# Turning a head's second negated maxima behind the next head's first scores, and rounding sample queries in fewer operations

## The chip, the cores and the metric

The kernel runs on one core of a Trainium2 chip. A core has TensorE (matmuls; its weight loads are listed apart as PEld), VectorE (DVE), ScalarE (ACT), GpSimd (POOL) and SyncE (SP), which here only issues DMAs. Each engine works through its own instructions in order; engines wait for each other by semaphores. Matmul results land in PSUM, everything else lies in SBUF or in DRAM. The metric is the device time of one execution in microseconds (us); the time before is the median of three runs.

## What is computed

One inference step of a trunk of two layers, for a prompt of 1024 positions and for 8 samples of 8 new positions each: a Mamba-2 layer, then a layer of multi-head latent attention (MLA), with the same weights for both groups. The change lies in the attention layer. For the prompt, with 16 heads, a latent of 256 and a rotary part of 32:

```python
def latent_partial(q_lat, q_pe, ckv, kpe, mask):
    s = (jnp.einsum('bqhc,bkc->bhqk', q_lat, ckv.astype(F32))
         + jnp.einsum('bqhr,bkr->bhqk', q_pe.astype(F32), kpe.astype(F32))) * MLA_SCALE
    if mask is not None:
        s = jnp.where(mask, s, NEG_INF)
    m = jnp.max(s, axis=-1)
    p = jnp.exp(s - m[..., None])
    return m, jnp.sum(p, axis=-1), jnp.einsum('bhqk,bkc->bhqc', p, ckv.astype(F32))
```

The samples use the same function over 16 pages of an old cache and their own new positions. Their queries in latent form are `absorb(q_nope, w_uk)`, a product with a head's 64 x 256 weights, beside the rotary part `q_pe`.

## The kernel before

**Number format.** Most operands of matmuls are written as a sum of two parts in a rounded 32-bit format (fp32r): `split` (L129, L130) has ScalarE round a source into the high part, and VectorE subtract it from the source into the low part. A product then takes three matmuls: high by high, low by high, high by low.

**Prompt heads.** `mla_heads` loops over 16 heads h. For each head there are 12 steps t; step t scores one block of 128 keys against a half qc of the queries (512): four steps for the first half, eight for the second. `qk` (L1246 to L1253) computes the transposed scores in PSUM (tile st, two buffers), and ScalarE takes the exponential twice, once rounded (th) and once in full (P); VectorE or GpSimd writes their difference tl (L1260). `pv` (L1277 to L1279) multiplies by the values two steps later.

The exponential needs the maximum of each query subtracted. This is done inside the score matmul: rows 96 and 97 of the transposed queries (qTh) hold the negated maxima as two parts, and the keys have ones there. So, one head ahead, `maxpass(h + 1, qc)` computes coarse scores (tile sc, L1214), and VectorE reduces them (L1217, L1219), negates the maxima (L1225, L1226, tile nm), TensorE turns them (L1229, tile nmp), VectorE copies the result to SBUF (L1231, nr), and two DMAs on SP's queue carry it through DRAM (L1233, nd) into rows 96 and 97 of qTh (L1234). `qk` of step t = 0 needs the rows of the first half, that of t = 4 those of the second.

**Units between the steps.** Beside `qk` and `pv`, each step takes some units of other work from a list: 6 units of `maxpass(h + 1, 0)` (a), 10 of `maxpass(h + 1, 1)` (b), and 4 to 16 of `prep(h + 2)` merged evenly into it: for every fourth head the values of four heads (vp), for every second the keys (kp), and for each head the query transposes (qT), the sample queries' transposes (qs) and the sample product (ql). The list is spread over the 12 steps: `while done < total * (t + 1) // 12`. The last two units of b are the negation and the turn. Within a step the order is `qk`, then units, then `pv` of two steps before.

**Sample queries.** In `prep_q` (L1176 to L1200) TensorE transposes a head's 64 sample queries (96 rows: 64 plain, 32 rotary) and the head's weights into one PSUM tile (qs). VectorE copies the queries (qsn, L1182), ScalarE the weights (wt, L1184). One unit later TensorE multiplies both (L1188, tile ql) and the two halves of the latent are split one after the other into qlh and qll. The rotary part goes from qsn into qpr in three copies: high, high again, low (L1197 to L1199).

**What sets the order.** In this stage the instructions of TensorE and GpSimd run in the order in which the program writes them. The order on VectorE, ScalarE and SP's queue is laid out ahead of time by a planner with a cost model. Tiles with several buffers are reused as soon as their readers are done; readers of one PSUM tile on different engines take turns. The PSUM tiles of the units share four buffers (tag sc). The gate of a head (gt, L1271) and the results (og_d, L1292) use SP's queue too.

Of the kernel before, what the change touches and what calls it, by code (L numbers as in the profile page):

```python
# [8 lines left out]
F32 = mybir.dt.float32  # L9
F32R = mybir.dt.float32r  # L10
AF = mybir.ActivationFunctionType
ALU = mybir.AluOpType
# [7 lines left out]
NT = 8  # L20
# [106 lines left out]
def split(k, hi, lo, src, eng=None):  # L127
    nc = k.nc
    nc.scalar.copy(hi, src)  # L129
    (eng or nc.vector).tensor_tensor(lo, src, hi.bitcast(F32), op=ALU.subtract)  # L130
# [895 lines left out]
class Heads:  # L1026
# [136 lines left out]
    def prep_q(self, h):  # L1163
        k, nc, sp = self.k, self.k.nc, self.sp
        hg, pr, j = h // 4, h // 2, h % 2
        if j == 0:
            self.load_q(pr)
        qh, ql = self.q_of(h)
        for c in range(2):
            p = self.wt(f"qT{h}{c}")  # L1170
            for i in range(4):
                nc.tensor.transpose(p[:96, i * 128 : i * 128 + 128], self.qt[:, 4 * c + i, 96 * j : 96 * j + 96], k.ident)
            cs = slice(512 * c, 512 * c + 512)
            split(k, qh[:96, cs], ql[:96, cs], p[:96])
            yield
        p = self.wt(f"qs{h}")  # L1176
        nc.tensor.transpose(p[:96, :64], self.qt[:64, 8, 96 * j : 96 * j + 96], k.ident[:64, :64])
        for c in range(2):
            nc.tensor.transpose(p[:64, 128 + c * 128 : 256 + c * 128],
                                self.wkr[:, c, 64 * (h % 4) : 64 * (h % 4) + 64], k.ident)  # L1180
        qsn = sp.tile([96, 64], F32, tag="qsn", name=f"qsn{h}", bufs=2)
        nc.vector.tensor_copy(qsn, p[:96, :64])  # L1182
        wt = sp.tile([64, 256], F32, tag="wt", name=f"wt{h}", bufs=2)
        nc.scalar.copy(wt, p[:64, 128:384])  # L1184
        yield
        pl = self.wt(f"ql{h}p")
        for c in range(2):
            nc.tensor.matmul(pl[:, c * 64 : c * 64 + 64], wt[:, c * 128 : c * 128 + 128], qsn[0:64],  # L1188
                             start=True, stop=True)
        for c in range(2):  # L1190
            src = pl[:, c * 64 : c * 64 + 64].rearrange("p (b t) -> p b t", t=NT)
            dh = k.qlh[:, c].rearrange("p b (h t) -> p b h t", t=NT)[:, :, h]
            dl = k.qll[:, c].rearrange("p b (h t) -> p b h t", t=NT)[:, :, h]
            split(k, dh, dl, src)
        src = qsn[64:96].rearrange("p (b t) -> p b t", t=NT)
        qv = k.qpr.rearrange("p b (h t) -> p b h t", t=NT)[:, :, h]
        nc.vector.tensor_copy(qv[0:32], src)  # L1197
        nc.vector.tensor_copy(qv[32:64], src)
        nc.vector.tensor_tensor(qv[64:96], src, qv[0:32].bitcast(F32), op=ALU.subtract)  # L1199
        yield  # L1200

    def maxpass(self, h, qc):
        k, nc, sp = self.k, self.k.nc, self.sp
# [96 lines left out]
def merge(*lists):  # L1300
    z = [((i + 0.5) / len(x), n, u) for n, x in enumerate(lists) for i, u in enumerate(x)]
    return [u for _, _, u in sorted(z, key=lambda e: e[:2])]


def mla_heads(k, hd, sm, early, st):
    k.tc.keep_in_program_order(k.nc.scalar.preload_act_table_set("natural_log_exp_and_others"))
    held, late = [], []

    def step(g):
        try:  # L1310
            next(g)
        except StopIteration:
            pass

    for h in range(MH):
        units = []
        if h == MH - 2:
            early.close()
            sm.begin(st, hd.psum)
        if h + 1 < MH:  # L1320
            a, b = hd.maxpass(h + 1, 0), hd.maxpass(h + 1, 1)
            units += [a] * 4 + [b, a, b, b, b, a] + [b] * 6
        if h + 2 < MH:
            g = hd.prep(h + 2)
            units = merge(units, [g] * hd.units(h + 2))
        if h + 2 == MH:
            g = sm.prefetch()
            units[PF:PF] = [g] * 2
            units += [g] * 2
        if h + 1 == MH:  # L1330
            sm.preload()
            flow = sm.flow()
            units = [flow] * FLOW
        total, done = len(units), 0
        for t in range(12):
            qc, jb = (0, t) if t < 4 else (1, t - 4)
            held.append((h, qc, jb, *hd.qk(h, qc, jb)))
            while done < total * (t + 1) // 12:
                step(units[done])
                done += 1  # L1340
            if len(held) > LEAD:
                hd.pv(*held.pop(0))
    for x in held:
        hd.pv(*x)
    return flow
# [447 lines left out]
def layer_mla(k):  # L1793
# [3 lines left out]
    with ExitStack() as st:  # L1797
# [29 lines left out]
        with tc.manual_schedule(engines={nc.tensor.engine, nc.gpsimd.engine}):  # L1827
            flow = mla_heads(k, hd, sm, early, st)
# [64 lines left out]
```

## Time and profile before

| | |
|---|---|
| time before, median of 3 runs | 2104.4 us (2102.95 to 2106.95) |
| span of the profiled execution, first to last instruction | 2095.4 us |
| mean granted TensorE clock over the span | 0.969 |
| instructions | 33766 |
| busy in the span: TensorE, weight loads, VectorE, ScalarE, GpSimd | 1948.3, 1763.6, 1340.1, 1043.3, 851.9 us |
| prompt heads, from the first head's first scores to the last head's steps | 1433 to 1815 us |

The profiled execution's own total time isn't listed beside its span; its span is 9.0 us shorter than the median of the runs.

A row of the profile in order of time reads: start, duration, engine, line, operation, tile written <- tiles read, shapes, count, and in brackets how long the engine was idle before it and what ended that. A row of a group reads: line, engine, operation, tiles, shapes, count, then busy time and mean duration in ns, then the engine's idle time before these instructions and what ended most of it. In a view of one tile, the last lines say for whom the engine sat idle before the tile's instructions (us, times). A row of a stretch gives its length, the busy time and count of each engine, the granted clock (1.00 is full speed) and what the DMAs did.

### The profile page before, as it was taken

Reading aid. Unit: us, or ns where it says so; the run is one execution under the profiler, and the core shown is the slowest. Engines: PE = TensorE matmul, PEld = TensorE weight load, DVE = VectorE, ACT = ScalarE, POOL = GpSimd, SP = SyncE. Lnnn points to the kernel's source line nnn. Section 1 sums busy time; section 2 is a strip of 40 time slices with the busy share of each in tenths; the row PEclk is TensorE's granted clock in tenths of the full one; section 3 lists DMA queues with packets and bytes.
Section 4 is the critical chain, followed back from the end, with each engine's and each line's share of the span. In section 5 each row is a group of like instructions: output and inputs, shape, how many; then the busy total and the mean of one; then the engine's idle time right before and its main releaser. Section 6 shows DMA issues by size and latency. Waiting matters only on the chain.

```text
span 2095.4 us, 33766 instructions
## 1 busy us (share of the span) xinstructions
PE 1948.3 (93%) x12001; PEld 1763.6 (84%) x12001; DVE 1340.1 (64%) x2838; ACT 1043.3 (50%) x2287; POOL 851.9 (41%) x1059
## 2 busy tenths in 40 slices
PE   6999999999999999789998999699999999889998
PEld 5898999899999998677787998698888888778887
DVE  4558676767676767865334314366787778776665
ACT  5455565556565656522114323234676667755552
POOL 0337564646664646744000001102343334765541
PEclk9999999999999999889999999899999989999999
DMA  4222324231324241635534342132111112464451
GB/s 144 56 59 64 111 66 115 56 114 57 105 66 115 56 115 46 208 122 192 183 124 133 124 152 63 52 108 68 48 55 52 43 37 61 133 197 131 142 152 40
DMA packets 187631, 207.61 MB, mean 99 GB/s; under 512 B 23260, under 2 KB 153064, under 8 KB 187080
## 3 DMA queue, kind: packets, MB, share of 16 engines
q1 hardware_dynamic: 182408, 185.67, 29.2%
q0 software_dynamic: 4976, 19.66, 3.0%
q8 instruction: 95, 1.56, 0.3%
q14 instruction: 72, 0.59, 0.1%
q10 hardware_dynamic: 80, 0.13, 0.0%
HBM read 152.10 MB, written 53.28 MB: 98 GB/s over the span
## 4 chain that ended last, share of the span: by engine, by line
PE 33%; DVE 9%; issue 4%; POOL 4%; DMA 3%; ACT 2%; SPq 0%; POOLq 0%; DVEq 0%; ACTq 0%
PE pq L100 5%; PE pob L100 5%; PE pj L88 4%; PE poa L100 2%; POOL kvl L1541 2%; PE pk L100 1%; PE p L100 1%; PE vp L88 1%; PE st L1246 1%; DVE tl L1260 1%; PE st L1248 1%; PE st L1247 1%; PE o L1277 1%; PE sc L1214 1%; PE kp L88 1%
## 5 line engine op out<-in xcount | busy, mean ns | idle before, releaser
L88 PE MATMUL pj<-xh,wih 128*128 128x384 f32 (+1 forms) x768 | 254.9, 336 | 10.9 <-ACT xh L235 6.6
L88 PE MATMUL pj<-xl,wih 128*128 128x384 f32 (+1 forms) x768 | 255.9, 333 | 0.0
L88 PE MATMUL pj<-xh,wil 128*128 128x384 f32 (+1 forms) x768 | 255.1, 332 | 0.0
L1260 POOL TENSOR_TENSOR tl<-P,th 128x384 fp32r<-128x384 f32 (+1 forms) x96 | 90.7, 945 | 181.0 <-ACT P L1258 138.5
L88 PEld LDWEIGHTS pj<-xh,wih 128*128 128x128 f32 x768 | 145.8, 191 | 12.5 <-ACT xh L235 7.5
L468 DVE SCALAR_TENSOR_TENSOR acc<-raw,vec,acc 128x1112 f32<-128x1112 f32 x96 | 147.0, 1535 | 11.9 <-ACT acc L465 11.1
L88 PEld LDWEIGHTS pj<-xh,wil 128*128 128x128 f32 x768 | 146.3, 190 | 0.6
L88 PEld LDWEIGHTS pj<-xl,wih 128*128 128x128 f32 x768 | 146.1, 190 | 0.5
L575 DVE TENSOR_SCALAR M<-M,tok 128x128 f32<-128x128 f32 (+1 forms) x288 | 116.6, 462 | 43.0 <-DMA M<-acs_d 35.7
L100 PE MATMUL pz<-wih,xh 128*128 128x256 f32 x504 | 143.0, 287 | 0.0
L100 PE MATMUL pz<-wil,xh 128*128 128x256 f32 (+1 forms) x504 | 142.8, 287 | 0.0
L1257 ACT ACTIVATE th<-st 128x512 fp32r<-128x512 f32 x192 | 94.1, 490 | 73.6 <-PE st L1253 54.7
L100 PE MATMUL pz<-wih,xl 128*128 128x256 f32 x448 | 128.1, 286 | 0.0
L130 DVE TENSOR_TENSOR wil<-wraw,wih 128x512 fp32r<-128x512 f32 x88 | 70.4, 802 | 65.7 <-ACT wih L129 63.1
L1541 POOL TENSOR_TENSOR kvl<-pgr,kvh 128x1024 fp32r<-128x1024 f32 x32 | 78.2, 2445 | 67.8 <-ACT kvh L1540 67.8
L100 PEld LDWEIGHTS pz<-wih,xh 128*128 128x128 f32 x504 | 96.0, 190 | 1.1
L577 ACT ACTIVATE M<-M 128x512 f32<-128x512 f32 (+1 forms) x72 | 43.8, 608 | 102.0 <-DVE M L575 101.7
L1258 ACT ACTIVATE P<-st 128x512 f32<-128x512 f32 x192 | 93.2, 486 | 0.0
L100 PEld LDWEIGHTS pz<-wil,xh 128*128 128x128 f32 (+1 forms) x504 | 92.9, 184 | 0.3
L663 POOL TENSOR_TENSOR y<-y,nw 128x256 f32<-128x256 f32 (+1 forms) x72 | 64.5, 896 | 70.2 <-ACT xD L662 69.7
L582 PEld LDWEIGHTS py<-xdt,M 128*128 128x128 f32 (+1 forms) x576 | 70.4, 192 | 19.8 <-DVE xdt L555 6.5
L100 PEld LDWEIGHTS pz<-wih,xl 128*128 128x128 f32 x448 | 85.4, 191 | 0.4
(819 smaller groups left out, 6461.6 us busy)
## 6 DMA issues: line engine op xcount, KB each, us to landing
wraw<-in_ssd_w_in SPq DMA_DIRECT2D x92, 256.0 KB
M<-acs_d SPq DMA_DIRECT2D x64, 256.0 KB
s<-in_state_ssm SPq DMA_DIRECT2D x32, 256.0 KB
y_d<-y SPq DMA_DIRECT2D x64, 128.0 KB
out_s_ssm<-s SPq DMA_DIRECT2D x32, 256.0 KB
wraw<-in_ssd_w_out SPq DMA_DIRECT2D x16, 512.0 KB
q_d<-qt SPq DMA_DIRECT2D x32, 192.0 KB
qp<-q_d SPq DMA_DIRECT2D x8, 768.0 KB
```

The lines of the kernel that those rows point to most:

```text
L88: nc.tensor.matmul(out, a, b, start=(i == 0), stop=(i == n - 1))
L100: nc.tensor.matmul(o, a, b, start=(j == 0), stop=(j == len(ops) - 1))
L130: (eng or nc.vector).tensor_tensor(lo, src, hi.bitcast(F32), op=ALU.subtract)
L468: nc.vector.scalar_tensor_tensor(acc, raw[:, j : j + n], k.convw[j][:, blk : blk + 1], acc, op0=ALU.mult, op1=ALU.add)
L575: nc.vector.tensor_scalar(M[:m, h, :m], M[:m, h, :m], tk[:, 0, 4 * g + h : 4 * g + h + 1], 0.0, op0=ALU.subtract, op1=ALU.min)
L577: nc.scalar.activation(M[:m, :, :m], M[:m, :, :m], AF.Exp)
L582: nc.tensor.matmul(py[:m, h * 64 : h * 64 + 64], M[:m, h, :m], xdt[:m, h * 64 : h * 64 + 64], start=True, stop=True)
L663: nc.gpsimd.tensor_tensor(y[:m], y[:m], nw[:m], op=ALU.mult)
L1257: nc.scalar.activation(th[:, :n], ps[:, :n], AF.Exp, scale=SCALE)
L1258: nc.scalar.activation(P[:, :n], ps[:, :n], AF.Exp, scale=SCALE)
L1260: eng.tensor_tensor(tl[:, :n], P[:, :n], th[:, :n].bitcast(F32), op=ALU.subtract)
L1541: nc.gpsimd.tensor_tensor(rl, raw, rh.bitcast(F32), op=ALU.subtract)
```

## The change

Two edits. The last unit of `maxpass(h + 1, 1)`, which turns the second half's negated maxima and sends them on, leaves the list of units: the list is one unit shorter, and the generator is kept (`turn`) and taken one step further in the next head, just after that head's first `qk`. And `prep_q` takes the rotary part straight from PSUM with one `split`, splits both halves of the latent in one operation each, and leaves the second copy of the rotary high part to one copy for all heads, issued at the start of head 14 (`rope_queries`).

```diff
-        qsn = sp.tile([96, 64], F32, tag="qsn", name=f"qsn{h}", bufs=2)
-        nc.vector.tensor_copy(qsn, p[:96, :64])
+        qsn = sp.tile([64, 64], F32, tag="qsn", name=f"qsn{h}", bufs=2)
+        nc.vector.tensor_copy(qsn, p[:64, :64])
+        qv = k.qpr[:, :, NT * h : NT * h + NT]
+        split(k, qv[0:32], qv[64:96], p[64:96, :64].rearrange("p (b t) -> p b t", t=NT))
         wt = sp.tile([64, 256], F32, tag="wt", name=f"wt{h}", bufs=2)
         nc.scalar.copy(wt, p[:64, 128:384])
         yield
...
-            nc.tensor.matmul(pl[:, c * 64 : c * 64 + 64], wt[:, c * 128 : c * 128 + 128], qsn[0:64],
+            nc.tensor.matmul(pl[:, c * 64 : c * 64 + 64], wt[:, c * 128 : c * 128 + 128], qsn,
                              start=True, stop=True)
-        for c in range(2):
-            src = pl[:, c * 64 : c * 64 + 64].rearrange("p (b t) -> p b t", t=NT)
-            dh = k.qlh[:, c].rearrange("p b (h t) -> p b h t", t=NT)[:, :, h]
-            dl = k.qll[:, c].rearrange("p b (h t) -> p b h t", t=NT)[:, :, h]
-            split(k, dh, dl, src)
-        src = qsn[64:96].rearrange("p (b t) -> p b t", t=NT)
-        qv = k.qpr.rearrange("p b (h t) -> p b h t", t=NT)[:, :, h]
-        nc.vector.tensor_copy(qv[0:32], src)
-        nc.vector.tensor_copy(qv[32:64], src)
-        nc.vector.tensor_tensor(qv[64:96], src, qv[0:32].bitcast(F32), op=ALU.subtract)
+        src = pl[:, :128].rearrange("p (c b t) -> p c b t", c=2, t=NT)
+        split(k, *(x[:, :, :, NT * h : NT * h + NT] for x in (k.qlh, k.qll)), src)
         yield
+
+    def rope_queries(self):
+        k, nc = self.k, self.k.nc
+        nc.scalar.copy(k.qpr[32:64], k.qpr[0:32].bitcast(F32))
...
-    held, late = [], []
+    held, turn = [], iter(())
...
-        units = []
+        units, b = [], iter(())
         if h == MH - 2:
             early.close()
+            hd.rope_queries()
             sm.begin(st, hd.psum)
         if h + 1 < MH:
             a, b = hd.maxpass(h + 1, 0), hd.maxpass(h + 1, 1)
-            units += [a] * 4 + [b, a, b, b, b, a] + [b] * 6
+            units += [a] * 4 + [b, a, b, b, b, a] + [b] * 5
...
             held.append((h, qc, jb, *hd.qk(h, qc, jb)))
+            if t == 0:
+                step(turn)
+                turn = b
```

## The prediction

> **What bounds the kernel now.** I read the page's first lines, then the stretch from 1433 to 1790 us, in which the heads run, by engine, then TensorE's idle time there, then single boundaries between heads in order of time. Page and busy time by stretch (columns: length, then PE, PEld, DVE, ACT, POOL busy, granted clock, DMA share, GB/s):
>
> ```profile
> PE 1948.3 (93%) x12001; PEld 1763.6 (84%) x12001; DVE 1340.1 (64%) x2838; ACT 1043.3 (50%) x2287; POOL 851.9 (41%) x1059
> ...
> 1433.00:1790.00 357.00, 334.22 (x1845) 289.36 (x1844) 280.44 (x696) 241.34 (x547) 129.85 (x126) 0.95 0.18 51
> ```
>
> TensorE is busy 334 of 357 us, VectorE 280, ScalarE 241: TensorE's program order is the clock of this stage, and its 23 idle us are what an edit can win. The view of the tile nmp (the turned maxima) on TensorE says where they are:
>
> ```profile
> L1229 PE MATMUL nmp<-ident,nm x29: 269/273/377, 1459.9 to 1788.7; 128*8 128x128 f32 x29
> its engine sat idle before it (us, times) until:
>   DVE nm L1226: 14.2, 11
>   DVE qll L130: 3.2, 4
> ```
>
> So 17.4 of the 23 us stand in front of one 0.27 us transpose, once at each of the 15 head boundaries (11 + 4). One boundary, TensorE then VectorE:
>
> ```profile
> 1476.43 0.44 PE L1214 MATMUL sc<-kTh,qTh 96*128 96x512 f32 x1
> ...
> 1478.47 0.28 PE L1253 MATMUL st<-mr 128*128 128x128 f32 x1
> 1480.78 0.27 PE L1229 MATMUL nmp<-ident,nm 128*8 128x128 f32 x1 [2.04 <-DVE nm L1226]
> 1480.81 0.42 PE L1277 MATMUL o<-th,Vh 128*128 128x384 f32 x1
> ...
> 1481.41 0.40 PE L1246 MATMUL st<-qTh,kTh 98*128 98x512 f32 x1
> 1481.65 0.40 PE L1247 MATMUL st<-qTl,kTh 98*128 98x512 f32 x1
> ...
> 1482.23 0.42 PE L1214 MATMUL sc<-kTh,qTh 96*128 96x128 f32 x1
> ```
> ```profile
> 1479.22 0.76 DVE L1219 CUSTOM_DVE_ANT_0 sc<-sc,mk,mx 128x512 f32<-128x512 f32 x1
> ...
> 1480.56 0.16 DVE L1226 SCALAR_TENSOR_TENSOR nm<-mx,nm 128x4 fp32r<-128x4 f32 x1
> ```
>
> The last score of the pass is ready at 1476.87, but VectorE, behind, takes it at 1479.22, and the transpose waits. What follows it, a value product (1480.81 to 1481.41) and the next head's first scores (to 1482.23), needs nothing of it.
>
> Idle time here costs twice. Stretches at half clock:
>
> ```profile
> 1482.10:1488.90 6.80, 6.80 (x30) 6.68 (x29) 3.74 (x10) 4.20 (x9) 1.93 (x2) 0.50 0.07 20
> 1512.80:1516.20 3.40, 3.40 (x14) 3.11 (x13) 1.26 (x4) 1.27 (x3) 0.00 (x0) 0.50 0.01 2
> 1577.70:1581.10 3.40, 3.40 (x13) 3.11 (x12) 0.92 (x4) 1.08 (x2) 0.00 (x0) 0.50 0.01 2
> 1669.80:1680.10 10.30, 9.79 (x39) 9.40 (x40) 5.14 (x18) 4.42 (x10) 2.28 (x2) 0.50 0.05 16
> 1704.00:1707.40 3.40, 3.40 (x15) 3.19 (x14) 1.22 (x5) 1.51 (x4) 0.00 (x0) 0.50 0.00 1
> 1724.40:1731.30 6.90, 6.59 (x21) 5.91 (x22) 1.77 (x7) 2.52 (x7) 1.31 (x2) 0.51 0.02 4
> ```
>
> Between 1455 and 1790 these six, 34.2 us, are all there is below full clock, and each begins within 2 us of such a wait (1480.78, 1511.35 and 1702.17 are quoted). The price:
>
> ```profile
> 1513.20 0.63 PE L1247 MATMUL st<-qTl,kTh 98*128 98x512 f32 x1
> 1513.63 0.63 PE L1248 MATMUL st<-qTh,kTl 98*128 98x512 f32 x1
> ```
>
> Start to start 0.43 us where 1481.41 to 1481.65 took 0.24: about 0.45 of such a stretch is lost, 15.4 us in all.
>
> **The change, part by part.**
>
> *The transpose behind the next head's first scores.* Same instructions, later place. It now comes after the value product (0.60) and the scores (0.82), 1.42 us of cover. The list of units is also one shorter and is spread again over the 12 steps. Three kinds of boundary follow.
>
> - h = 0, 4, 8, 12 (the four that wait for qll): the last score stays in step 10, the cover exceeds the wait of 0.8 (3.2 in four). Gone: −3.2.
> - h odd, seven: the last score moves from step 10 to step 11, just before the value product, so the cover counts from its end. From the rows: reading it 0.76, two negations of 0.16, some 0.2 between them, 1.3 us against 1.4. Nothing remains if VectorE is free; if it is still 2.35 us behind (1476.87 to 1479.22), some 2.3 remain, as now. What held it up there goes in part with the second edit; I take a remainder of 0.5 at h = 1, 5, 9, where VectorE also splits weights, and 0.2 at the other four, 2.3 in all (bounds 0 and 16). h = 14 likewise loses its small wait. These eight have 17.4 − 3.2 − 3 × 0.85 = 11.65 now, so −11.65 + 2.3 = −9.4.
> - h = 2, 6, 10: here the query transposes, the maxima's transpose and the sample product stand in a row:
>
> ```profile
> 1510.09 0.41 PE L1179 MATMUL qs<-ident,w 128*64 128x128 f32 x2
> 1511.35 0.27 PE L1229 MATMUL nmp<-ident,nm 128*8 128x128 f32 x1 [0.85 <-DVE nm L1226]
> 1511.58 0.66 PE L1188 MATMUL ql4p<-qsn,wt 64*128 64x64 f32 x4
> ...
> 1606.20 0.27 PE L1229 MATMUL nmp<-ident,nm 128*8 128x128 f32 x1 [0.85 <-DVE nm L1226]
> ...
> 1702.17 0.27 PE L1229 MATMUL nmp<-ident,nm 128*8 128x128 f32 x1 [0.85 <-DVE nm L1226]
> ```
> ```profile
> 1510.92 0.21 DVE L1182 COPY qsn<-qs 96x64 f32<-96x64 f32 x1
> 1511.16 0.36 ACT L1184 COPY wt<-qs 64x256 f32<-64x256 f32 x1 [0.71 <-DVE qsn L1182]
> 1441.53 0.58 ACT L129 CAST kTh<-kp 64x512 fp32r<-64x512 f32 x1 [3.23 <-DVE kTl L130]
> ```
>
> Take the transpose away and the sample product still waits for wt, which ends at 1511.52. Idle is not 0.85 but 1.08, before the second edit.
>
> *Its DMAs.* The store and the load of the row (SP's queue) move back by the same 1.4 us:
>
> ```profile
> 1556.08 0.27 PE L1229 MATMUL nmp<-ident,nm 128*8 128x128 f32 x1 [0.80 <-DVE qll L130]
> ...
> 1556.69 0.27 SPq L1233 DMA_DIRECT2D nd<-nr  x1
> 1557.90 0.22 SPq L1234 DMA_DIRECT2D qTh<-nd  x1
> 1562.59 0.45 SPq L1271 DMA_DIRECT2D gt<-g_d  x1
> ...
> 1556.71 0.40 PE L1246 MATMUL st<-qTh,kTh 98*128 98x512 f32 x1
> ...
> 1562.30 0.40 PE L1246 MATMUL st<-qTh,kTh 98*128 98x512 f32 x1
> ```
>
> The store lands 1.2 us after its issue (the load waits for it); give the load the same. From a transpose 0.8 behind the head's start at 1556.71: 0.6 to the store's issue (1556.08 to 1556.69 now), 1.2, 1.2, so 3.8 us; the rows are first used at 1562.30, 5.6 us behind the start. Slack 1.8: priced 0. The scores of the first half, which read the same tile meanwhile, did so before as well.
>
> *Sample queries.* For each head VectorE loses the two casts of the rotary part and one of two latent differences; the rotary difference reads PSUM now. ScalarE trades two latent casts for one of double width and a rotary one. From the groups (busy us, mean ns), one of the casts and the difference:
>
> ```profile
> L1199 DVE TENSOR_TENSOR qpr<-qsn,qpr 32x64 fp32r<-32x64 f32 x14 | 10.0, 712 | 0.4
> ...
> L1197 DVE CAST qpr<-qsn 32x64 fp32r<-32x64 f32 x14 | 7.6, 542 | 0.5
> ```
>
> With the difference cut to qsn's 0.21, 14 x (0.71 − 0.21 + 0.54), 14.6 us or about one per head leaves VectorE, and more with the rest. It had 77 idle us anyway, so it counts only in the backlog above. But ScalarE's wt now stands behind a copy and a difference on the same PSUM tile. Such readers take turns here: the cast at 1441.53 reads other partitions than the difference it waits for. So qsn, copy, difference, wt run in a chain. The two new links cost some 0.2 each by qsn's 0.21, with handovers 0.5 to 0.6. At h = 2, 6, 10 this is on TensorE's path: idle 1.6 instead of 0.85, 3 × 0.75 = +2.3. Elsewhere value products and scores stand between.
>
> [...]
>
> *The one copy for all heads at h = 14,* 32 x 1024 on ScalarE: at most the 1.05 us of
>
> ```profile
> L1540 ACT CAST kvh<-pgr x1: 1051/1051/1051, 1785.6 to 1785.6; 128x1024 fp32r<-128x1024 f32 x1
> ```
>
> ScalarE idles longer than that around a head's start; if not, +1. Taken: 0.
>
> *The clock.* Four stretches follow boundaries that lose their wait: 6.8 + 3.4 + 10.3 + 6.9 = 27.4 us, × 0.45 = −12.3. The two of 3.4 at h = 2 and 10 stay, and with 1.6 us idle I take three of 5.1: (15.3 − 6.8) × 0.45 = +3.8.
>
> **Sum:** −3.2 − 9.4 + 2.3 − 12.3 + 3.8 = −18.8. The span is 2095.4, 9.0 below the median of 2104.4; the profiled execution's own total isn't shown, and I carry the 9.0 over: 2085.6.
>
> **Rivals.**
>
> 1. *The waits go, the clock doesn't follow* (0.18). Speaks for it: several waits of 0.8 to 1.3 us have no half clock behind them. Against: none of the six stretches stands without one. Then −18.8 + 8.5 = −10.3: 2094. [...]
> 2. *The wait moves along* (0.13). VectorE stays behind, the later last score eats the cover, and the seven odd heads keep their wait behind the first scores. Then only −3.2 + 2.3 remains, and the clock as before or +3.8: 2103 to 2107.
> 3. *The rows come late* (0.12), the slower side. SP's queue is in order; if the load is put behind the gate's load, which waited until 1562.59, it is issued at 1563.04 and lands at 1564.25, 1.95 us after the scores want it. The odd heads and h = 14, 15 have no projection before that point: 9 × 1.95 = 17.6, and half clock after such waits by up to 3.1 each (6.8 × 0.45), say 14. That turns −18.8 into +13: 2117. It decides as soon as the path of 3.8 us grows by more than 1.8. Against: the gate's load becomes possible over 4 us after the row's load in the rows above.
> 4. *Nothing remains, and the clock stays full* (0.05): −17.4 − 15.4 gives 2072.
>
> **How the numbers follow.** My forecast has 0.52, own range 2078 to 2093. The range 2071 to 2106 takes in rivals 1, 4 and most of 2 and leaves out 3. About 0.2% (4.2 us) can be told from no change: faster 0.52 + 0.18 + 0.05; of rival 2 most is no change, with 0.02 on either side: faster 0.77, same 0.09, slower 0.14.
>
> **What would show it.** In the new profile the tile nmp has almost no idle time before it; ql waits for wt at three boundaries by 1.6 us; half clock is left only behind those; the first scores of each second half wait for no DMA; the rotary rows are gone from VectorE. I am wrong if TensorE idles before nmp behind the first scores, or before the scores of step 4, or if half clock appears without idle time ahead of it.

## The result, and the profile after

The changed kernel takes 2081.15 us (median of four runs, 2076.63 to 2084.15), the kernel before 2103.68 beside it (2101.3 to 2106.95): a ratio of 0.9898, 95% interval 0.9877 to 0.9919. The prediction was 2085.6. A second set of runs gave 2080.1 against 2097.64, 0.9924 (0.9901 to 0.9947). The time came out as forecast; the experiments show that most of the gain has another source than the prediction said.

The page of the kernel after, and the stretch from its first head's first scores to its last head's (columns as before: length, busy time of PE, PEld, DVE, ACT, POOL, granted clock, DMA):

```profile
PE 1939.1 (93%) x12001; PEld 1750.3 (84%) x12001; DVE 1325.8 (64%) x2790; ACT 1043.0 (50%) x2288; POOL 852.6 (41%) x1059
...
1428.87:1771.47 342.60, 327.83 (x1843) 281.31 (x1843) 264.76 (x651) 242.30 (x550) 130.38 (x126) 0.97 0.20 53
```

The same stretch of the kernel before:

```profile
1433.42:1790.45 357.03, 334.25 (x1845) 289.42 (x1845) 280.05 (x694) 241.72 (x549) 129.85 (x126) 0.95 0.18 51
```

The stage is 14.4 us shorter: TensorE's idle time falls from 22.8 to 14.8 (−8.0), its busy time, for the same matmuls, by 6.4: less half clock. The span (2077.3) is 18.1 shorter; 4.6 of it lie ahead of the first head, where of all that changed only the sample queries of the first two heads are prepared. In the second profile of the same kernel the heads begin at 1432.28 and take 340.2, so at least 3.4 of those 4.6 belong to the execution, not to the change.

Behind what TensorE waits now, from the waits of the kernel after in that stretch (us in total, times, longest), and the tile nmp:

```profile
PE sc L1212 <- DVE mx L1217: 3.5, 1, 3.5
PE st L1244 <- ACT P L1256: 2.0, 2, 1.7
PE st L1244 <- DMA qTh<-nd: 1.9, 3, 0.7
PE ql8p L1190 <- ACT wt L1186: 1.8, 1, 1.8
PE ql12p L1190 <- ACT wt L1186: 1.8, 1, 1.8
PE ql4p L1190 <- ACT wt L1186: 1.8, 1, 1.8
PE nkp L1408 <- DVE nk L1405: 0.7, 1, 0.7
PE o L1277 <- POOL tl L1258: 0.7, 1, 0.7
...
PE nmp L1227 <- DVE nm L1224: 0.2, 1, 0.2
```

The longest wait, 3.5 us in the first head, is the same in the kernel before (3.5 there, too). Of 17.4 us in front of the maxima's transpose, 0.2 are left. In their place stand 5.5 before three sample products, 1.9 behind DMAs at three first scores of a head, and near the end some 0.7 to 2 each behind ScalarE, VectorE and GpSimd. One of the three sample products, and the chain ahead of it, in order of time on TensorE, VectorE and ScalarE:

```profile
1500.78 0.41 PE L1179 MATMUL qs<-ident,w 128*64 128x128 f32 x2
1503.02 0.65 PE L1190 MATMUL ql4p<-qsn,wt 64*128 64x64 f32 x4 [1.84 <-ACT wt L1186]
```
```profile
1501.77 0.21 DVE L1182 COPY qsn<-qs 64x64 f32<-64x64 f32 x1
1502.35 0.22 DVE L130 TENSOR_TENSOR qpr<-qs,qpr 32x64 fp32r<-32x64 f32 x1
```
```profile
1502.02 0.20 ACT L129 CAST qpr<-qs 32x64 fp32r<-32x64 f32 x1 [0.88 <-DVE qsn L1182]
1502.60 0.36 ACT L1186 COPY wt<-qs 64x256 f32<-64x256 f32 x1 [0.38 <-DVE qpr L130]
```

The four readers of the tile stand in a row, as the prediction had it, and the weights are last. The stretches at half clock in the kernel after:

```profile
1437.00:1440.40 3.40, 3.40 (x11) 2.85 (x11) 1.87 (x7) 1.01 (x3) 3.34 (x5) 0.50 0.46 98
1505.30:1508.70 3.40, 3.40 (x17) 3.37 (x17) 1.73 (x6) 2.27 (x5) 0.64 (x1) 0.50 0.04 7
1594.00:1600.80 6.80, 6.80 (x27) 6.36 (x27) 2.02 (x7) 2.22 (x5) 0.13 (x1) 0.50 0.01 4
1686.20:1693.00 6.80, 6.58 (x24) 6.15 (x25) 1.86 (x6) 2.17 (x6) 0.00 (x0) 0.50 0.01 1
```

The first has its like in the kernel before (at 1441). The other three, 17.0 us instead of 34.2, begin within 2.3 us of the end of one of the three waits of 1.84. In the second profile of this kernel (the run c1 below) two of the three have half clock behind them, 13.7 us in all, and the third, just as long, has none. Last, a wait that was not foreseen, TensorE and then SP's queue:

```profile
1558.98 0.27 PE L1227 MATMUL nmp<-ident,nm 128*8 128x128 f32 x1
1565.81 0.47 PE L1244 MATMUL st<-qTh,kTh 98*128 98x512 f32 x1 [0.65 <-DMA qTh<-nd]
```
```profile
1557.36 0.39 SPq L1159 DMA_DIRECT2D qp<-q_d  x1
...
1560.30 0.43 SPq L1231 DMA_DIRECT2D nd<-nr  x1
1564.18 0.25 SPq L1232 DMA_DIRECT2D qTh<-nd  x1
```

Those are the rows of the first half. Their store stands behind the load of new queries (qp, 768 KB in the list of DMA issues) and takes 3.9 us to the next issue, where the rows of the second half took 1.2. In the kernel before the same two issues were 4.9 us apart, at the boundary that the prediction shows (its first scores start at 1481.41):

```profile
1473.04 0.42 SPq L1233 DMA_DIRECT2D nd<-nr  x1
...
1477.94 0.25 SPq L1234 DMA_DIRECT2D qTh<-nd  x1
```

There the scores came 3.5 us behind the load's issue; without the 2.04 us before the transpose it would have been 1.4, less than the 1.6 (1564.18 to 1565.81) that the load takes here.

### The profile page after: what moved, and what is told of

Same layout as the page of the kernel before. It is cut to its first block, busy times and chain, and to the rows that moved or that the text cites. A ratio compares the mean times of both kernels' runs of the same rounds, so it can differ in the third digit from the quotient of the medians.

```text
span 2077.3 us, 33714 instructions
## 1 busy us (share of the span) xinstructions
PE 1939.1 (93%) x12001; PEld 1750.3 (84%) x12001; DVE 1325.8 (64%) x2790; ACT 1043.0 (50%) x2288; POOL 852.6 (41%) x1059
## 4 chain that ended last, share of the span: by engine, by line
PE 58%; DVE 15%; DMA 10%; issue 7%; POOL 5%; ACT 4%; SPq 1%; POOLq 0%; DVEq 0%; ACTq 0%
PE pj L88 12%; PE pz L100 9%; PE pq L100 5%; PE pob L100 5%; DMA M<-acs_d 4%; PE poa L100 4%; DVE M L575 3%; DVE acc L468 3%; POOL kvl L1543 2%; PE py L582 2%; PE sc L1212 1%; PE st L1244 1%; PE o L1275 1%; PE st L1246 1%; PE st L1245 1%
## 5 line engine op out<-in xcount | busy, mean ns | idle before, releaser
L1258 DVE TENSOR_TENSOR tl<-P,th 128x512 fp32r<-128x512 f32 x96 | 74.3, 774 | 22.4 <-ACT P L1256 22.1
```

The source lines that it names most:

```text
L1258: eng.tensor_tensor(tl[:, :n], P[:, :n], th[:, :n].bitcast(F32), op=ALU.subtract)
```

## The experiments

The theory on record: the waits go because the turn is covered by a value product and the first scores, the second edit only frees VectorE, and the clock follows the waits. The rival that the result suggested: it is the second edit that lets VectorE catch up, and the turn's new place is not needed.

**Each edit alone.** The kernel before with the turn's move only:

```diff
-            units += [a] * 4 + [b, a, b, b, b, a] + [b] * 6
+            units += [a] * 4 + [b, a, b, b, b, a] + [b] * 5
...
+            if t == 0:
+                step(turn)
+                turn = b
```

> Only the turn is moved; the sample queries are as before. Theory A (the turn's cover and the relief of VectorE both count): the transpose has a wait left at the odd heads, since VectorE still does the rotary casts, 0.3 to 1 us each; at h = 2, 6, 10 the sample product waits about 1.1 us for the weights' copy, not 1.84. Idle time of TensorE before nmp 3 to 7 us, time 2082 to 2092 us. Theory B (the cover alone does it): no wait before nmp, time at or below the changed kernel's 2081 us, because the query chain is short too. Theory C (the relief of VectorE is what counted): the waits before nmp stay near 17 us and the time near 2104.

And the kernel after without that move, so with the new sample queries only:

```diff
-            units += [a] * 4 + [b, a, b, b, b, a] + [b] * 5
+            units += [a] * 4 + [b, a, b, b, b, a] + [b] * 6
...
-            if t == 0:
-                step(turn)
-                turn = b
```

> Only the sample queries are changed; the turn stays at the end of its head. Theory A: the wait before nmp at the odd heads falls from 11.3 us in seven to some 5 to 8, as VectorE is less behind; at h = 2, 6, 10 the sample product waits longer for the weights' copy, by about 1 us each. Half clock stays behind the longer waits. Time 2094 to 2106 us. Theory B (cover alone): nothing gained, and the longer query chain costs 3 to 6 us: 2104 to 2110. Theory C (relief alone): the waits before nmp nearly vanish and the time is 2085 or less.

The turn alone: 2085.09 us, 0.9925 (0.9907 to 0.9943). The queries alone: 2074.33, 0.9876 (0.9854 to 0.9898). Of the theories on record for the turn, A has the time right (2082 to 2092), and its waits before nmp are a little smaller than it said (2.7 us). For the queries C is the nearest (2.9 us left before nmp, the time below 2085), and A's 2094 to 2106 fails. The gains overlap, they don't add up: either edit takes most of the odd heads' waits, and the queries alone are at least as fast as both together. To make sure of that, the changed kernel and the queries alone ran once more side by side:

> The changed kernel once more, beside the next one on the same chip. Theory (the second edit carries the gain, and the move of the turn takes a little back): slower than the kernel with the second edit alone, by 2 to 8 us. Rival (both are equal within what can be told): less than 2 us apart.

> The second edit alone once more: 0.985 to 0.990 of the time of the kernel before, 2 to 8 us below the changed kernel on this chip. Rival: less than 2 us apart.

2080.1 (2078.1 to 2086.32) against 2074.05 (2069.92 to 2077.72): no run of the one reaches into those of the other. As ratios to the kernel before they are 0.9924 (0.9901 to 0.9947) and 0.9893 (0.987 to 0.9917). So on top of the queries, the turn's move costs about 6 us, inside the 2 to 8 that were expected. The waits of the queries alone show where:

```profile
PE nmp L1227 <- DVE nm L1224: 2.9, 4, 0.8
PE st L1244 <- DMA qTh<-nd: 1.5, 2, 1.0
...
PE ql4p L1190 <- ACT wt L1186: 0.5, 1, 0.5
```

At h = 2, 6, 10 the transpose, still between the query transposes and the sample product, takes 0.85 of the wait, and 0.46 is left for the product: 1.3 each, where both edits together have 1.84. There is less half clock, too: between the heads 1 and 14 two stretches of 3.4 us in one profile and none in the other, against 17.0 and 13.7 us with both edits.

**Why the queries alone suffice.** At the boundary from h = 1 to 2 in the kernel before, VectorE and then GpSimd:

```profile
1472.66 0.85 DVE L1197 CAST qpr<-qsn 32x64 fp32r<-32x64 f32 x1
1473.54 0.19 DVE L1198 CAST qpr<-qsn 32x64 fp32r<-32x64 f32 x1
1473.76 1.21 DVE L1199 TENSOR_TENSOR qpr<-qsn,qpr 32x64 fp32r<-32x64 f32 x1
...
1476.98 1.49 DVE L130 TENSOR_TENSOR w<-w,w 128x512 fp32r<-128x512 f32 x1
```
```profile
1472.09 1.37 POOL L1291 TENSOR_TENSOR og<-og,rl 64x512 f32<-64x512 f32 x1 [1.14 <-PE qs L1179]
1473.54 1.35 POOL L1260 TENSOR_TENSOR tl<-P,th 128x512 fp32r<-128x512 f32 x1
1476.61 1.31 POOL L1260 TENSOR_TENSOR tl<-P,th 128x384 fp32r<-128x384 f32 x1 [1.73 <-PE st L1253]
```

Two equal casts take 0.85 and 0.19 us; the slow one ends at 1473.51, just behind GpSimd's 1473.46. The difference ends at 1474.97, behind 1474.89. The weights' difference ends 0.55 after GpSimd's 1477.92. All three started while a GpSimd instruction was running. It is so at all seven odd heads (the cast 0.83 to 0.85, the difference 1.2); at the other seven heads no GpSimd instruction is running and the difference takes 0.22. The weights' difference takes 0.68 (the queries alone) and 0.69 (the kernel after, at 1473.36) where it starts ahead of GpSimd. In all these rows VectorE's operation lasts until the GpSimd instruction that was there first has ended: the long casts end 0.04 or 0.05 us after it, the long differences 0.08 or 0.09, the weights' difference, in all five heads that have one, 0.55 or 0.56. What holds the operations up the rows don't show. The queries alone, same boundary, VectorE:

```profile
1472.91 0.68 DVE L130 TENSOR_TENSOR w<-w,w 128x512 fp32r<-128x512 f32 x1
1473.51 0.75 DVE L1217 CUSTOM_DVE_ANT_0 sc<-sc,mk,mx 128x512 f32<-128x512 f32 x1
```

The casts are gone, the rotary difference has its source in PSUM (0.22 in all 14 heads; in the kernel after too, where 11 of them start while a GpSimd instruction runs on for 0.3 to 0.75 us), and everything behind them is earlier: the weights' difference starts 0.12 us ahead of GpSimd's next instruction (1473.03), and the last reduction starts 0.08 after the score's end (1472.99 + 0.44), where it was 2.35 late.

To see which part of the second edit does this, each half of it was built without the turn's move. The rotary part alone (the latent split stays in two halves):

```diff
-        src = pl[:, :128].rearrange("p (c b t) -> p c b t", c=2, t=NT)
-        split(k, *(x[:, :, :, NT * h : NT * h + NT] for x in (k.qlh, k.qll)), src)
+        for c in range(2):
+            src = pl[:, c * 64 : c * 64 + 64].rearrange("p (b t) -> p b t", t=NT)
...
+            split(k, dh, dl, src)
```

> Of the second edit the rotary part alone: the rotary part is split straight from PSUM, so the casts and the difference that read SBUF on VectorE (542, 185 and 712 ns in the mean, drawn out while GpSimd is busy) are gone; the latent is still split in two halves. Theory (these casts are what puts VectorE behind): the wait before nmp at the odd heads is gone but for 0 to 2 us in seven, time 2078 to 2086 us. Rival (the two halves of the latent, whose casts wait for each other, are what delays the maxima): the waits at the odd heads stay at 8 us or more, time 2095 to 2106 us.

The latent part alone (the rotary part stays in three copies from qsn):

```diff
-        for c in range(2):
...
-            split(k, dh, dl, src)
+        src = pl[:, :128].rearrange("p (c b t) -> p c b t", c=2, t=NT)
+        split(k, *(x[:, :, :, NT * h : NT * h + NT] for x in (k.qlh, k.qll)), src)
```

> Of the second edit the latent part alone: both halves of the latent split in one operation each; the rotary casts stay on VectorE as before. Theory (the rotary casts put VectorE behind): the waits before nmp at the odd heads stay at 8 to 12 us in seven; the 0.8 at h = 0, 4, 8, 12 may change; ratio to the kernel before 0.995 to 1.001. Rival (both parts give relief alike, and either does): the waits at the odd heads fall below 4 us, ratio 0.992 or less.

The rotary part alone: 2076.95, 0.9895 (0.9865 to 0.9924); before nmp 2.9 us are left, 0.85 at each of h = 2, 6, 10 and 0.3 at h = 14, nothing at the odd heads. The latent part alone: 2098.05, 0.9985 (0.9968 to 1.0002), no difference that shows. The waits of both came as the theory had them, and the first time is a little below its 2078 to 2086. The trace of the latent part keeps the drawn-out operations and the waits, VectorE and TensorE:

```profile
1475.69 1.21 DVE L1196 TENSOR_TENSOR qpr<-qsn,qpr 32x64 fp32r<-32x64 f32 x1
...
1478.91 1.49 DVE L130 TENSOR_TENSOR w<-w,w 128x512 fp32r<-128x512 f32 x1
```
```profile
PE nmp L1226 <- DVE nm L1223: 18.8, 15, 2.1
```

So the rotary operations on VectorE, and what they pushed into GpSimd's way, carry the odd heads' waits. The turn alone takes all but 2.7 us of the waits with the casts still there; in its trace the cast is drawn out as before (1.03 us at this boundary), while the rotary and the weights' difference take 0.22 and 0.67. In their stead a difference tl on VectorE, 0.69 where it is free, is drawn out to 1.76 (at 1471.45). It moved the meeting as well as covering it, and how much each is worth there was not told apart.

**Does the clock follow the waits?** The changed kernel with seven extra matmuls of 128 x 512 ahead of the three sample products; what they write is overwritten by the product, so nothing of the result changes:

```diff
         pl = self.wt(f"ql{h}p")
+        if h % 4 == 0 and h > 0:
+            for _ in range(7):
+                nc.tensor.matmul(pl, k.kvh[:, 0, 0:128], k.kvh[:, 0, 0:512], start=True, stop=True)
```

> The changed kernel, with seven matmuls of 128x512 put in front of the sample product at h = 2, 6, 10, where TensorE waits 1.84 us for the weights' copy; their result is overwritten by the product. They take some 1.65 us at full clock, so the wait is filled and the product starts when it did. Theory A (idle time in a window lets the clock fall): the half clock behind these three places (3.4 + 6.8 + 6.8 us in the profiled execution) is gone, the stage is 5 to 8 us shorter, time 2072 to 2079 us. Rival (the half clock has another cause): stretches of half clock stay in the stage from head 1 to head 14, and the time is 2080 to 2085.

Its wait and clock:

```profile
PE ql8p L1193 <- ACT wt L1186: 0.2, 1, 0.2
...
1446.40:1767.30 320.90, 314.12 (x1815) 268.76 (x1813) 251.86 (x623) 234.60 (x533) 122.73 (x117) 1.00 0.20 52
1767.30:1774.10 6.80, 6.80 (x24) 6.12 (x25) 2.19 (x7) 2.48 (x8) 3.12 (x4) 0.50 0.04 7
```

Useless work in place of the wait (0.2 us of it are left), and the clock is full over 321 us. From the first scores of h = 1 to those of h = 14 it takes 288.8 us, the changed kernel 296.1 and 294.4 in its two profiles. So the idle time is the cause of the half clock behind these waits, as theory A has it, and the 0.45 that the prediction took per us (17.0 × 0.45 = 7.7, 13.7 × 0.45 = 6.2) is about what comes back (7.3 and 5.6). This is one profiled execution; unfilled, five of six such waits in the changed kernel's two profiles have half clock behind them, filled none of three. The next long wait (1.92, behind ScalarE's P) brings the next stretch, at 1767.30. In total time it is 2077.44, 0.989 (0.9871 to 0.9909), not to be told from the changed kernel's first ratio.

**How much slack do the rows have?** The turn two steps later:

```diff
-            if t == 0:
+            if t == 2:
                 step(turn)
```

> The changed kernel, with the turn taken two steps later in the next head, behind the scores of step 2 instead of step 0. Theory A (3.8 us from the transpose to landed rows, wanted 5.6 us behind the head's start): the transpose stands some 3 us behind the head's start, the rows land 0.5 to 1.5 us after the scores of step 4 want them, in the nine heads without projections in front; TensorE waits there for the DMA, 5 to 13 us in all, and half clock follows some of them: 2088 to 2102 us. Rival (the path has much more room than that): no wait for the DMA at step 4, 2079 to 2084 us.

2119.61, 1.0096 (1.0073 to 1.0118): slower than the kernel before, and more than theory A had (2088 to 2102). The waits of TensorE, one of them with the chain behind it, TensorE and SP:

```profile
PE st L1244 <- DMA qTh<-nd: 21.0, 13, 2.6
...
1460.82 0.27 PE L1227 MATMUL nmp<-ident,nm 128*8 128x128 f32 x1
1465.58 0.47 PE L1244 MATMUL st<-qTh,kTh 98*128 98x512 f32 x1 [2.16 <-DMA qTh<-nd]
```
```profile
1461.93 0.27 SPq L1231 DMA_DIRECT2D nd<-nr  x1
1463.01 0.45 SPq L1269 DMA_DIRECT2D gt<-g_d  x1
1463.55 0.39 SPq L1232 DMA_DIRECT2D qTh<-nd  x1
```

Ten of the 13 waits stand at step 4, 18.6 us, where 5 to 13 were expected; three are those of the first half. So the rows of the third rival can come late, and the gate's load stands here between their store and their load, as it said. These rows give the price: from the transpose to the scores 4.76 us here and 4.6 to 5.1 at the other nine, of which the load takes 1.7 to 2.3 from issue to use. The prediction had given it 1.2.

**Where the weights' copy stands.** The changed kernel with ScalarE's copy of the weights ahead of the rotary split:

```diff
-        split(k, qv[0:32], qv[64:96], p[64:96, :64].rearrange("p (b t) -> p b t", t=NT))
         wt = sp.tile([64, 256], F32, tag="wt", name=f"wt{h}", bufs=2)
         nc.scalar.copy(wt, p[:64, 128:384])
+        split(k, qv[0:32], qv[64:96], p[64:96, :64].rearrange("p (b t) -> p b t", t=NT))
```

> The changed kernel with the weights' copy in front of the rotary split, so that it follows the queries' copy alone. Theory (the two new links of the chain, rotary copy and difference, are on TensorE's path at h = 2, 6, 10): the wait in front of the sample product falls from 1.84 to about 1.2 us at these three; with less half clock behind them the stage from head 1 to head 14 is 2 to 6 us shorter than the changed kernel's 294 to 296 us. Rival (VectorE's late start on the queries' copy sets it): still 1.6 us or more.

```profile
PE ql8p L1190 <- ACT wt L1184: 1.3, 1, 1.3
```

From the waits: 1.25 instead of 1.84, so the theory holds, and the two links of the chain cost the 0.6 that the prediction gave them. From head 1 to head 14 it takes 287.3 us, 7.1 to 8.8 less than the changed kernel where 2 to 6 were expected: in this execution there is no half clock behind the three waits. The time, 2076.06, 0.9876 (0.9852 to 0.99), is no worse than the changed kernel's, and the difference is less than these runs can tell.

**All that was learned in one kernel.** The queries without the turn's move, the weights' copy first, and the last unit of the first half's pass (its turn) earlier, ahead of the query load in SP's queue, with an empty unit added to the list of every fourth head:

```diff
-            units += [a] * 4 + [b, a, b, b, b, a] + [b] * 5
+            units += [a] * 4 + [b, a, b, b, a, b] + [b] * 6
...
-            units = merge(units, [g] * hd.units(h + 2))
+            units = merge(units, [g] * hd.units(h + 2) + [iter(())] * (h % 4 == 2))
```

> The second edit alone, with three small moves: the weights' copy stands in front of the rotary split, so it no longer takes its turn behind it; at h = 2, 6, 10 the preparation units come a little earlier in the list, so that value product and scores stand between the query transposes and the sample product; and the last unit of the first half's maxima comes one unit earlier. Theory: the waits left in front of nmp and the sample product at h = 2, 6, 10 (0.85 + 0.46 us each) and for the first half's rows (0.5 to 1.0 us at h = 1, 5) go, and the half clock behind them: 3 to 9 us below the second edit alone. Rival (they turn up elsewhere, at the next unit that VectorE holds up): less than 2 us below it.

2068.35 (2064.68 to 2073.07), 0.9859 (0.9834 to 0.9883): 11.8 us under the changed kernel on the same chip, where no run of the one reaches into those of the other, and 5.7 under the queries alone (2074.05), inside the 3 to 9 that were expected, though there the single runs overlap. The small moves were not tried one by one. Its waits in the heads up to 1760.9:

```profile
PE nmp L1227 <- DVE nm L1224: 0.9, 2, 0.6
PE ql4p L1190 <- ACT wt L1184: 0.8, 1, 0.8
...
1443.40:1760.90 317.50, 311.69 (x1814) 270.36 (x1813) 247.01 (x636) 237.77 (x539) 124.81 (x124) 0.99 0.20 53
```

No first scores wait for a DMA any more: the first half's rows are stored ahead of the load of new queries. The sample products wait 0.8. Half clock is left only at the start of this stretch (1443.4 to 1446.8, the first head's, as at 1441 in the kernel before and 1437.0 in the kernel after); from there to its end the clock is full.

## Why the prediction was right, and where it was not

- **The time.** 2085.6 forecast, 2081.15 measured, inside its own range of 2078 to 2093. In part this is luck, as two errors work against each other. The heads gained 14.4 in the pair of profiles where 18.8 was forecast (16.8 in the second profile). And the 9.0 us between the profiled span and the median were not overhead: the kernel after has 1.8 between its span of 2077.3 and its own run of 2079.06. By the same 1.8 the profiled execution of the kernel before took some 2097 us, less than any of its four runs (an estimate); most of the 4.6 us ahead of the heads are of the same kind.
- **"These eight have … 11.65 now, so −11.65 + 2.3": right in size, wrong in cause.** The waits went (17.4 to 0.2). But the step credits the cover of 1.42 us, and the queries alone, without that cover, lose the odd heads' waits too. The step that failed is "It had 77 idle us anyway, so it counts only in the backlog": that backlog was the wait. The prediction listed VectorE's 542 and 712 ns for the casts and the difference and took them for the operations' own length; beside GpSimd's rows they are short operations (0.18 and 0.22 us where no GpSimd instruction runs) that stand still. Had it asked why a 32 x 64 cast takes 0.85 us once and 0.19 right after, the second edit could have been seen as the larger one.
- **The remainder of 2.3 at the odd heads** measured 0.2, for the same reason.
- **The three sample products:** 1.6 each forecast, 1.84 found. The chain of readers is as described and worth 0.6; the rest is mostly that VectorE takes qsn 0.58 us after the transposes' end (1501.19 to 1501.77), 0.42 in the rows of before that the sum used. The program has the readers of the tile take turns in every kernel here (in the rows of the tile qs above each starts 0.03 to 0.13 us after the end of the one before); a kernel without these turns was not tried.
- **A term that the sum lacks: the rows of the first half,** 1.9 us at three boundaries. The part "Its DMAs" follows the store and the load of the row that moves and not those of the other row, whose lateness lay under the 2.04 us wait that the change took away. It appears with the queries alone as well (1.5), where no unit moves, so it is not the turn's new place that brings it out; the last kernel, which issues this store earlier, has none of it.
- **Slack 1.8 us at step 4, priced 0:** the price held, no scores of a second half wait. The slack was nearer 1: 0.62 and 1.20 to the two issues (1566.64, 1567.26, 1568.46 in the trace after), then about 2.0 for the load, 3.8 behind a turn that lies 0.83 after the head's start, against 5.65. With the turn two steps later the rows do come late, as in the third rival: 1.0096.
- **The clock:** forecast 15.3 us of half clock left behind three waits, found 17.0. The first rival (the clock does not follow) falls with the filled waits. The second (the wait moves along) needed VectorE to stay behind, and it did not: 0.2 us are left in front of nmp. The fourth (nothing remains) falls with the 14.8 us of idle time and 17.0 of half clock that are left.
- **Not foreseen:** from h = 14 on, waits behind ScalarE's P, the new keys and GpSimd are 1.6 us longer in total than in the kernel before. The longest of them, ScalarE and then TensorE:

```profile
1766.92 1.05 ACT L1542 CAST kvh<-pgr 128x1024 fp32r<-128x1024 f32 x1 [1.54 <-DMA pgr<-in_cache_ckv,ptidx]
```
```profile
1769.00 0.39 PE L1244 MATMUL st<-qTh,kTh 98*128 98x256 f32 x1 [1.70 <-ACT P L1256]
```

ScalarE waits for a part of the samples' old cache, and the exponentials stand behind its cast; the kernel before has the like (a cast at 1785.58 behind 1.23 us, then a wait of 0.85). Why it costs more here is open. The copy for all heads is not the cause of these waits: it ends at 1747.09, over 15 us earlier. It can answer for 0.2 at ql15p, and the wait for the new keys (0.7) is there in the turn-only kernel too (1.3), which has no such copy.

Summed by the prediction's own terms: idle −17.4 + 2.3 + 4.8 = −10.3 forecast, −17.2 + 5.7 (the sample products, with 0.2 at ql15p) + 1.9 + 1.6 = −8.0 measured; clock −8.5 forecast, −6.4 measured.

## What to carry to other kernels

When one engine waits for another that is "behind", look for short operations of that engine with two very different durations (here one cast with 0.19 and 0.85 us), and lay them beside GpSimd's instructions: taking away or moving the one that collides may be worth more than hiding the wait. When a wait of 2 us is taken away, list everything that becomes ready less than 2 us ahead of its end, the DMAs of rows that are not touched included. And test two edits one by one even when both together win: here the second alone was faster than both.

## What the runs showed of the hardware that was not expected

- **Some of VectorE's operations lasted until a GpSimd instruction had ended.** 0.19 against 0.85 us for a 32 x 64 cast from SBUF, 0.22 against 1.21 for a difference, 0.68 against 1.49 for a 128 x 512 difference, the drawn-out ones each ending 0.04 to 0.56 us after the GpSimd instruction that ran at its start. The mean of the weights' difference over the heads is 1298 ns before, 858 after and 811 with the queries alone.
- **Half clock stood behind waits of 0.85 to 2.15 us, but not behind all of them.** Of the three equal waits of 0.85 in the kernel before, two (1511.35, 1702.17) have half clock behind them and one (1606.20) has none. The four stretches of the kernel after start 68.3, 88.7 and 92.2 us apart, 20, 26 and 27 times 3.41 us (249.2 us over 73), and last one or two times that; the six of the kernel before that the prediction lists start 9, 19, 27, 10 and 6 times 3.41 apart: in these two profiles the changes of the clock lie on a grid of 3.41 us. In the 3.41 us ahead of the three later ones TensorE was idle for 1.1, 1.8 and 1.6 us. In the second profile of the kernel after (the run c1) the third wait of 1.84, the one without half clock behind it, falls across an edge of the grid, with 0.7 us idle in one 3.41 and 1.1 in the next. In one execution of the queries alone, two of the three waits of 1.3 brought 3.4 us of half clock, in the other none of the three did; where a wait falls on the grid would explain this, and might explain part of the scatter of some 4 us to either side between runs; neither was tried by itself. In the first head TensorE waits 3.5 us ahead of the stretch; ahead of the others the longest wait was 2.15 us in the kernel before and 1.84 in the kernel after, so in these rows half clock came without a whole 3.41 us of idle time ahead of it.
